# Attention scores in the array's row halves, grouped values in its column halves, steps by query tile

## The chip, the core and the metric

The kernel runs on one core of a Trainium2 chip. The metric is the time of one execution on the device in microseconds (us). The core's engines each run their own queue of instructions in order and wait for each other on semaphores: PE (TensorE, the matmul array), VectorE (DVE in the profile), ScalarE (ACT), GpSimd (POOL), and SyncE (SP), whose queue issues nearly all loads. Matmul results land in PSUM, eight banks of 128 partitions by 512 floats. An f32 matmul is two passes over the array and so two MATMUL records in the trace.

## The reference

A transformer block: modulation of the input by a condition vector, two attentions side by side, and a mixture of 32 experts, followed by a second block with a retention layer and a feed-forward net. The change touches the two attentions over 256 queries and 512 keys:

```python
def gqa_attention(q, k, v, q_block):          # 8 heads of 64, 2 key/value heads
    def block(qi):
        s = jnp.einsum('bhgqd,bkhd->bhgqk', qi, k) * scale
        p = jax.nn.softmax(s, axis=-1)
        return jnp.einsum('bhgqk,bkhd->bqhgd', p, v)
...
def diff_attention(q, k, v, lam, sub_g, lambda_init, q_block):   # 4 heads, two score maps of 64
    def block(qi):
        s = jnp.einsum('bhcqd,bkhcd->bhcqk', qi, k) * scale
        p = jax.nn.softmax(s, axis=-1)
        a = p[:, :, 0] - lam * p[:, :, 1]
        return jnp.einsum('bhqk,bkhe->bqhe', a, v)
    ...
    o = rms_norm(o, sub_g) * (1.0 - lambda_init)
```

The eight grouped heads are four pairs here: pair `c` holds head `c` of key/value head 0 and of key/value head 1 (`j`). Each head has 64 dimensions, so a score contracts over 64 only, half the array's 128 rows; a grouped value product has 64 output rows, half its columns.

## The kernel before

`attention_block` does everything from the first normalisation to the router. Weights come in 1 MB tiles; each is split by ScalarE (`hi`, line 141) and VectorE (`lo`, line 142), and a projection is three matmuls per tile (`hi,hh`, `hi,hl`, `lo,hh`, line 593). A scheduler orders each engine's instructions from their priorities and dependencies; the source gives the priorities. PE works through the projections of the difference attention (`kbT`, `vd`, `qd`) in the gaps of the grouped attention.

`attend` runs over `heads`, in the grouped attention eight (`c`, `j`), in the difference attention four. Step `i` issues the scores of head `i` (both query tiles `qt`), the transposes of head `i-1`, and the value product of head `i-2`, and calls `ada_step` (below). A grouped score uses rows `64*j` to `64*j+63` of `qT` and `kaT` and goes to bank `sc` (one bank). A difference score runs over 128 rows, with a `qd` in which the other half is zero (line 453, memset on GpSimd); two of them per query tile go to banks from the common pool `bank()`. `soft` takes the row maximum on VectorE (line 509), the exponential with sum on ScalarE (line 512), the reciprocal on VectorE (line 513). Grouped heads are scaled on ScalarE (line 530); difference heads are combined on VectorE (lines 536 to 538). The transposes go to bank `t`, and ScalarE copies them to `pTs` (line 520). The grouped value product writes `o[:64, :256]` (line 555), 256 columns over four key chunks, and ScalarE copies it into `mix` (line 557). The difference product (line 560) is followed by a sum of squares, an inverse root on VectorE (`rst`, `rsy`, lines 156 to 165), its spread over the columns (lines 289, 290), and `mix` on VectorE (line 568).

`Columns` is the modulation stream: it turns the condition vector into shifts and scales. A group is eight loads of 512 KB (two buffers); VectorE multiplies each by its column and adds it to `acc` (line 190 for the first, line 192 for the others), and after the eighth a `finish` sums over the partitions with eight one-column matmuls on PE (line 203) into bank `s`, from which VectorE adds the bias (line 205). There is one `acc` tile. `ada_step` hands out these steps over 30 places in the attention, at a low priority:

```python
for _ in range(min(len(todo) - slots[1] + slots[1] * slots[0] // ADA_PLACES, len(todo))):
    with tc.high_priority(offset=-LOW1):
        todo.pop(0).step((lambda: bank1("s")) if todo else None)
```

Behind the attention stand the output projection `w_o` (line 238), the router, and the experts (line 918), whose weights SyncE loads as soon as PE has freed their tiles.

Of the kernel before, what the change touches and what calls it, by code (L numbers as in the profile page):

```python
# [8 lines left out]
F32 = mybir.dt.float32  # L9
# [284 lines left out]
def attention_block(tc, g):  # L294
# [4 lines left out]
    with ExitStack() as es:  # L299
# [151 lines left out]

        qd = g.hp.tile([128, 4, 2, 256], F32, tag="h2", name="qd")
        nc.gpsimd.memset(qd, 0.0)
# [45 lines left out]
        pend = {}  # L499

        def scores(qa, ka, kind):
            b = bank1("sc") if kind == "g" else bank()
            pe.matmul(out=b, lhsT=qa, rhs=ka, start=True, stop=True)
            return b
# [11 lines left out]
        def transposed(p, pT, qt):  # L516
            b = bank1("t")
            for k in range(4):
                pe.transpose(out=b[:, k * 128:(k + 1) * 128], in_=p[:, k * 128:(k + 1) * 128], identity=g.ident)
            s.copy(out=pT[:, :, qt * 128:(qt + 1) * 128], in_=b.rearrange("p (k q) -> p k q", k=4))  # L520

        def stage_scores(heads, i):
            kind, c, j = heads[i]
            out = []
            for qt in range(2):
                qs = slice(qt * 128, (qt + 1) * 128)
                if kind == "g":
                    r = slice(64 * j, 64 * j + 64)
                    p, z = soft(scores(qT[r, c, qs], kaT[r, :], kind))
                    s.activation(out=p, in_=p, func=ACTF.Copy, scale=z)  # L530
                else:
                    pz = []
                    for m in range(2):
                        pz.append(soft(scores(qd[:, c, m, qs], kbT[:, c], kind)))
                    (p, z), (p1, z1) = pz
                    v.tensor_tensor(out=z1, in0=z1, in1=nlam, op=ALU.mult)
                    v.tensor_scalar(out=p, in0=p, scalar1=z, scalar2=None, op0=ALU.mult)
                    v.scalar_tensor_tensor(out=p, in0=p1, scalar=z1, in1=p, op0=ALU.mult, op1=ALU.add)
                out.append(p)
            pend[i] = out  # L540

        def stage_T(heads, i):
            pT = at.tile([128, 4, 256], F32, tag="pTs", name="pTs")
            for qt, p in enumerate(pend[i]):
                transposed(p, pT, qt)
            pend[i] = pT

        def stage_pv(heads, i):
            kind, c, j = heads[i]
            pT = pend.pop(i)  # L550
# [1561 lines left out]
```

## Time and profile before

| | us |
|---|---|
| median of 3 runs | 2090.07 |
| least and greatest | 2088.04, 2090.89 |
| the profiled execution | 2090.91 |
| its span in the trace | 2089.2 |
| first grouped score | 100.68 |
| first difference score | 192.30 |
| PE busy over the span | 1951.1 (93%) |

The trace is of one execution. Times of rows count from the start of its span, in us; a row of the timeline gives start, duration, engine, line, operation, output <- inputs, tile shape and count, and in brackets how long the engine had been idle before and what ended that. Durations of pipelined matmuls overlap: the step from one start to the next is what one costs. The chain of work that ended last lies in the second block, so the stretch of the change is read from the tables of stretches and the timelines.

### The profile page before, as it was taken

What the parts mean: (1) busy time and instruction counts of PE and PEld (TensorE: products, weight loads), DVE (VectorE), ACT (ScalarE), POOL (GpSimd) and SP (SyncE); (2) the same over time, 40 slices, a digit from 0 to 9 for tenths busy, and PEclk for the clock granted to TensorE, in tenths of its full rate; (3) what the DMA queues carried; (4) which work ended last, traced back from release to release, by engine and by line L of the source; (5) the groups of instructions that cost most, each with busy time, mean ns of one, the idle gap of its engine ahead of it and who ended that gap; (6) DMA issues with size and microseconds to landing.
All of it is one profiled execution on the core that took longest, in us unless ns stands there. A gap on an engine that the chain in (4) does not pass through costs nothing. (4 is left out here: it accounts for less than half of the span.)

```text
span 2089.2 us, 29010 instructions
## 1 busy us (share of the span) xinstructions
PE 1951.1 (93%) x11166; PEld 1246.5 (60%) x11166; DVE 1125.1 (54%) x2378; ACT 648.0 (31%) x1135; POOL 59.2 (3%) x92
## 2 busy tenths in 40 slices
PE   6999989999999989999998997999999999899998
PEld 3856844444333333332333326888999999599998
DVE  5865765132222212221222127999898978768863
ACT  3464311000000000000000004446677645256542
POOL 0000000000000000000000000000001002100000
PEclk9999989999999999999999998999999999799999
DMA  8656559999999999999999994667857778655651
GB/s 315 223 162 221 207 224 365 405 379 375 421 421 421 421 421 420 422 421 421 421 421 421 421 414 160 228 221 273 301 213 249 271 286 296 211 186 192 223 182 61
DMA packets 101757, 643.40 MB, mean 308 GB/s; under 512 B 11584, under 2 KB 12880, under 8 KB 34288
## 3 DMA queue, kind: packets, MB, share of 16 engines
q1 hardware_dynamic: 94176, 613.46, 75.1%
q0 software_dynamic: 6624, 26.76, 3.8%
q8 instruction: 89, 1.46, 0.3%
q10 hardware_dynamic: 816, 1.30, 0.2%
q14 instruction: 52, 0.43, 0.1%
HBM read 626.79 MB, written 14.68 MB: 307 GB/s over the span
## 5 line engine op out<-in xcount | busy, mean ns | idle before, releaser
L918 PE MATMUL hc<-w,xe 128*64 128x512 f32 (+1 forms) x2008 | 476.1, 598 | 54.1 <-DMA w<-in_w_in_dram 54.0
L918 PEld LDWEIGHTS hc<-w,xe 128*64 128x64 f32 (+1 forms) x2008 | 142.4, 138 | 375.3 <-issue 218.4
L142 DVE TENSOR_TENSOR lo<-w,hi 128x1024 fp32r<-128x1024 f32 x238 | 289.1, 1219 | 75.0 <-ACT hi L141 74.0
L141 ACT CAST hi<-w 128x1024 fp32r<-128x1024 f32 x238 | 249.0, 1049 | 253.0 <-PE b L241 156.7
L240 PE MATMUL b<-h2h,hi 128*128 128x256 f32 x896 | 254.6, 285 | 10.7 <-ACT h2h L1729 9.1
L938 DVE COPY hs<-hc 128x512 f32<-128x512 f32 x33 | 22.8, 691 | 448.8 <-PE hc L918 448.8
L241 PE MATMUL b<-h2l,hi 128*128 128x256 f32 x896 | 254.5, 285 | 0.2
L242 PE MATMUL b<-h2h,lo 128*128 128x256 f32 x896 | 253.9, 284 | 0.0
L918 PE MATMUL yb<-w,hb 128*64 128x512 f32 (+1 forms) x1024 | 252.6, 604 | 0.5 <-DMA w<-in_w_out_dram 0.5
L240 PEld LDWEIGHTS b<-h2h,hi 128*128 128x128 f32 x896 | 169.8, 190 | 13.3 <-ACT h2h L1729 9.3
L241 PEld LDWEIGHTS b<-h2l,hi 128*128 128x128 f32 x896 | 169.7, 190 | 4.0 <-issue 1.1
L242 PEld LDWEIGHTS b<-h2h,lo 128*128 128x128 f32 x896 | 169.7, 190 | 0.4 <-issue 0.4
L936 ACT COPY hs<-hc 128x512 f32<-128x512 f32 x33 | 19.3, 585 | 464.2 <-PE hc L918 464.2
L918 PEld LDWEIGHTS yb<-w,hb 128*64 128x64 f32 (+1 forms) x1024 | 66.8, 137 | 127.5 <-issue 119.5
L192 DVE SCALAR_TENSOR_TENSOR acc<-w,c,acc 128x1024 f32<-128x1024 f32 x77 | 98.4, 1278 | 12.0 <-DMA w<-in_ada_w_dram 11.4
L240 PE MATMUL b<-ah,hi 128*128 128x256 f32 x352 | 100.3, 286 | 0.0
L242 PE MATMUL b<-ah,lo 128*128 128x256 f32 x352 | 99.9, 284 | 0.2 <-DVE lo L142 0.2
L241 PE MATMUL b<-al,hi 128*128 128x256 f32 x352 | 99.4, 283 | 0.0
L981 ACT COPY ys<-yb 64x512 f32<-64x512 f32 (+1 forms) x32 | 18.5, 578 | 243.1 <-PE yb L918 243.1
L900 PEld LDWEIGHTS gb<-S,h 128*128 128x128 f32 x544 | 66.7, 197 | 37.2 <-issue 25.8
L1009 DVE TENSOR_TENSOR yacc<-sc,yacc 128x512 f32<-128x512 f32 x68 | 46.7, 688 | 66.5 <-PE sc L1007 66.5
L900 PE MATMUL gb<-S,h 128*128 128x128 f32 (+1 forms) x544 | 74.9, 289 | 1.2 <-DVE S L891 1.2
(523 smaller groups left out, 3061.1 us busy)
## 6 DMA issues: line engine op xcount, KB each, us to landing
w<-in_w_in_dram SPq DMA_DIRECT2D x252, 1024.0 KB, 13.1
w<-in_w_out_dram SPq DMA_DIRECT2D x128, 1024.0 KB, 14.5
w<-in_ffn_up_dram SPq DMA_DIRECT2D x44, 1024.0 KB, 5.0
w<-in_ada_w_dram SPq DMA_DIRECT2D x72, 512.0 KB, 5.0
w<-in_ret_w_in_dram SPq DMA_DIRECT2D x24, 1024.0 KB, 5.1
w<-in_ffn_down_dram SPq DMA_DIRECT2D x22, 1024.0 KB, 5.1
w<-in_w_ada_dram SPq DMA_DIRECT2D x32, 512.0 KB, 4.5
w<-in_ada_w_dram POOLq DMA_DIRECT2D x24, 512.0 KB, 4.8
```

Of the source, the lines that this page charges most:

```text
L141: self.nc.scalar.copy(out=hi, in_=w)
L142: self.nc.vector.tensor_tensor(out=lo, in0=w, in1=hi.bitcast(F32), op=ALU.subtract)
L192: v.scalar_tensor_tensor(out=self.acc, in0=w, scalar=cc, in1=self.acc, op0=ALU.mult, op1=ALU.add)
L240: pe.matmul(out=o, lhsT=w[0][:, sl], rhs=a[0][:, k], start=first, stop=False)
L241: pe.matmul(out=o, lhsT=w[0][:, sl], rhs=a[1][:, k], start=False, stop=False)
L242: pe.matmul(out=o, lhsT=w[1][:, sl], rhs=a[0][:, k], start=False, stop=last)
L900: g.got = pe.matmul(out=b[:, k * 128:k * 128 + n], lhsT=g.h2[:, t, d * 128:(d + 1) * 128], rhs=S[:, t, :n], start=(t == 0), stop=(t == 1))
L918: g.got = pe.matmul(out=on, lhsT=x, rhs=w[:, n * 512:n * 512 + 512], start=first, stop=last)
L936: s.copy(out=h, in_=hc[e][n])
L938: v.tensor_copy(out=h, in_=hc[e][n])
L981: s.copy(out=o, in_=i)
L1009: v.tensor_tensor(out=y, in0=b, in1=y, op=ALU.add)
```

## The change

The scores of both heads of a pair (grouped), or of both score maps of a head (difference), are issued one after the other on the array's upper and lower 64 rows and into different banks: grouped ones to `sc` and `s`, difference ones to two banks of the common pool. `qd` has no zero half any more, and one copy per query tile fills it. A step is now a query tile of a pair or head: `attend` runs eight steps per kind, with the transposes one step and the value product two steps behind. The grouped value product alternates between the column halves for `j` = 0 and 1, 128 query columns each; `mix` is copied once per pair. The difference product has 128 columns twice instead of 256 once. Each head's transposed weights have a tile of their own. `ada_step` is called with other numbers: 17 of 30 places in the grouped attention (15 before) and 10 in the difference attention (9 before). Lines from about 600 on are eight lower after the change.

```diff
--- before.py
+++ after.py
@@ -448,9 +448,7 @@
         qT, kbT, vd = (g.mw.tile([128, 2048], F32, tag="w", name=n) for n in ("qT", "kbT", "vd"))
         o24 = qT[:, 1024:].rearrange("p (i j t) -> p i j t", i=2, j=2)
         qT = qT[:, :1024].rearrange("p (c t) -> p c t", c=4)
-
-        qd = g.hp.tile([128, 4, 2, 256], F32, tag="h2", name="qd")
-        nc.gpsimd.memset(qd, 0.0)
+        qd = g.hp.tile([128, 4, 256], F32, tag="h2", name="qd")
         kbT, vd = (x.rearrange("p (c t) -> p c t", c=4) for x in (kbT, vd))
         va = pa.tile([128, 4, 128], F32, name="va")
         kaT = pa.tile([128, 512], F32, name="kaT")
@@ -496,12 +494,7 @@
         mix = g.sqp.tile([128, 8, 256], F32, tag="sq", name="mix")
         at = es_a.enter_context(tc.tile_pool(name="at", bufs=2))
 
-        pend = {}
-
-        def scores(qa, ka, kind):
-            b = bank1("sc") if kind == "g" else bank()
-            pe.matmul(out=b, lhsT=qa, rhs=ka, start=True, stop=True)
-            return b
+        bo = {}
 
         def soft(b):
 
@@ -513,51 +506,49 @@
             v.reciprocal(out=z, in_=z)
             return p, z
 
-        def transposed(p, pT, qt):
+        def transposed(p, j):
             b = bank1("t")
             for k in range(4):
                 pe.transpose(out=b[:, k * 128:(k + 1) * 128], in_=p[:, k * 128:(k + 1) * 128], identity=g.ident)
-            s.copy(out=pT[:, :, qt * 128:(qt + 1) * 128], in_=b.rearrange("p (k q) -> p k q", k=4))
-
-        def stage_scores(heads, i):
-            kind, c, j = heads[i]
-            out = []
-            for qt in range(2):
-                qs = slice(qt * 128, (qt + 1) * 128)
-                if kind == "g":
-                    r = slice(64 * j, 64 * j + 64)
-                    p, z = soft(scores(qT[r, c, qs], kaT[r, :], kind))
+            pT = at.tile([128, 4, 128], F32, tag=f"pT{j}", name="pTs")
+            s.copy(out=pT, in_=b.rearrange("p (k q) -> p k q", k=4))
+            return pT
+
+        def stage_scores(kind, c, qt):
+
+
+            q, ka = (qT, kaT) if kind == "g" else (qd, kbT[:, c])
+            bs = [bank1("sc"), bank1("s")] if kind == "g" else [bank() for _ in range(2)]
+            for j, b in enumerate(bs):
+                r = slice(64 * j, 64 * j + 64)
+                pe.matmul(out=b, lhsT=q[r, c, qt * 128:(qt + 1) * 128], rhs=ka[r], start=True, stop=True)
+            pz = [soft(b) for b in bs]
+            if kind == "g":
+                for p, z in pz:
                     s.activation(out=p, in_=p, func=ACTF.Copy, scale=z)
-                else:
-                    pz = []
-                    for m in range(2):
-                        pz.append(soft(scores(qd[:, c, m, qs], kbT[:, c], kind)))
-                    (p, z), (p1, z1) = pz
-                    v.tensor_tensor(out=z1, in0=z1, in1=nlam, op=ALU.mult)
-                    v.tensor_scalar(out=p, in0=p, scalar1=z, scalar2=None, op0=ALU.mult)
-                    v.scalar_tensor_tensor(out=p, in0=p1, scalar=z1, in1=p, op0=ALU.mult, op1=ALU.add)
-                out.append(p)
-            pend[i] = out
-
-        def stage_T(heads, i):
-            pT = at.tile([128, 4, 256], F32, tag="pTs", name="pTs")
-            for qt, p in enumerate(pend[i]):
-                transposed(p, pT, qt)
-            pend[i] = pT
-
-        def stage_pv(heads, i):
-            kind, c, j = heads[i]
-            pT = pend.pop(i)
-            o = bank1("o" if kind == "g" or c % 2 == 0 else "sc")
+                return [p for p, _ in pz]
+            (p, z), (p1, z1) = pz
+            v.tensor_tensor(out=z1, in0=z1, in1=nlam, op=ALU.mult)
+            v.tensor_scalar(out=p, in0=p, scalar1=z, scalar2=None, op0=ALU.mult)
+            v.scalar_tensor_tensor(out=p, in0=p1, scalar=z1, in1=p, op0=ALU.mult, op1=ALU.add)
+            return [p]
+
+        def stage_pv(kind, c, qt, pTs):
+            if qt == 0:
+                bo[c] = bank1("o" if kind == "g" or c % 2 == 0 else "sc")
+            o, qs = bo[c], slice(qt * 128, (qt + 1) * 128)
             if kind == "g":
-
                 for k in range(4):
-                    pe.matmul(out=o[:64, :256], lhsT=va[:, k, 64 * j:64 * j + 64], rhs=pT[:, k], start=(k == 0), stop=(k == 3))
-                r = slice(64 * j, 64 * j + 64)
-                s.copy(out=mix[r, c], in_=o[:64, :256])
+                    for j in range(2):
+                        r = slice(64 * j, 64 * j + 64)
+                        pe.matmul(out=o[r, qs], lhsT=va[:, k, r], rhs=pTs[j][:, k], start=(k == 0), stop=(k == 3))
+                if qt == 1:
+                    s.copy(out=mix[:, c], in_=o[:, :256])
             else:
                 for k in range(4):
-                    pe.matmul(out=o[:, :256], lhsT=vd[:, k, 128 * c:128 * c + 128], rhs=pT[:, k], start=(k == 0), stop=(k == 3))
+                    pe.matmul(out=o[:, qs], lhsT=vd[:, k, 128 * c:128 * c + 128], rhs=pTs[0][:, k], start=(k == 0), stop=(k == 3))
+                if qt == 0:
+                    return
                 o2, osb = (o24[:, c % 2, j] for j in range(2))
                 s.activation(out=o2, in_=o[:, :256], func=ACTF.Square)
                 s.activation(out=osb, in_=o[:, :256], func=ACTF.Copy, scale=g.subln)
@@ -567,16 +558,19 @@
                 spread(g, at, r, o[:, 256:])
                 v.tensor_tensor(out=mix[:, 4 + c], in0=osb, in1=o[:, 256:], op=ALU.mult)
 
-        def attend(heads):
-            n = len(heads)
-            for i in range(n + 2):
-                if i < n:
-                    stage_scores(heads, i)
-                if 0 <= i - 1 < n:
-                    stage_T(heads, i - 1)
-                if 0 <= i - 2 < n:
-                    stage_pv(heads, i - 2)
-                ada_step(2 if i % 2 else 1)
+        def attend(kind):
+
+
+            pend, pT = {}, {}
+            for i in range(10):
+                if i < 8:
+                    pend[i] = stage_scores(kind, *divmod(i, 2))
+                if 0 <= i - 1 < 8:
+                    pT[i - 1] = [transposed(p, j) for j, p in enumerate(pend.pop(i - 1))]
+                if i >= 2:
+                    stage_pv(kind, *divmod(i - 2, 2), pT.pop(i - 2))
+                if kind == "g" or i % 2:
+                    ada_step(2 if i % 4 else 1)
 
         def project(n, toks):
 
@@ -632,7 +626,7 @@
                             in0=qo[t].rearrange("p (j c d) -> p j c d", j=2, d=64),
                             in1=bc(r[:, 8 * t:8 * t + 8], 2, 64).rearrange("p (j c) d -> p j c d", j=2), op=ALU.mult)
             to_T(q2, qT[:, :, t * 128:(t + 1) * 128])
-        attend([("g", c, j) for c in range(4) for j in range(2)])
+        attend("g")
 
         bs = project(512, (0, 1, 2, 3))
         for t in range(4):
@@ -657,15 +651,13 @@
             for c in range(4):
                 pe.transpose(out=b[:, c * 128:(c + 1) * 128], in_=q2[:, c * 128:(c + 1) * 128], identity=g.ident)
             b = b.rearrange("p (c q) -> p c q", c=4)
-            for m in range(2):
-                r = slice(64 * m, 64 * m + 64)
-                s.copy(out=qd[r, :, m, t * 128:(t + 1) * 128], in_=b[r])
+            s.copy(out=qd[:, :, t * 128:(t + 1) * 128], in_=b)
 
         for i in range(20, 24, 2):
             t = g.hw.tile([128, 2, 2048], F32, tag="h", name="hw")
             for j in range(2):
                 ws.stream.load(i + j, t[:, j])
-        attend([("d", h, 0) for h in range(4)])
+        attend("d")
         for i in (17, 18, 24):
             ws.stream.ahead(i, g.mw)
         ws.stream.extend(g.mw, 3, 25, 13 + 32 * 12 - 1)
```

Three places in the order of the instructions. A row has its engine's line, operation, output <- input, shape, and a count where it repeats. First PE around the second finish of the modulation stream (`ones,acc`); before, bank `s` serves finishes alone:

```order
L593 MATMUL b<-lo,hh 128x512
L503 MATMUL sc<-kaT,qT 128x512
L519 MATMUL t<-ident,p 128x128 x4
L203 MATMUL s<-ones,acc_854 128x1 x8
L593 MATMUL b<-hi,hl 128x512
```

After, a score into `s` stands close behind the finish, without the score of its pair in front of it:

```order
L587 MATMUL b<-hi,hl 128x512
L203 MATMUL s<-ones,acc_858 128x1 x8
L587 MATMUL b<-hi,hh 128x512
L587 MATMUL b<-lo,hh 128x512
L524 MATMUL s<-kaT,qT 128x512
```

The score into `s` has moved behind the finish; its partner into `sc` is elsewhere in the queue.

Second, PE at the fourth finish and the first difference scores (`kbT,qd`), before:

```order
L203 MATMUL s<-ones,acc_1135 128x1 x8
L658 MATMUL t<-ident,qo 128x128 x4
L503 MATMUL b<-kbT,qd 128x512 x2
L658 MATMUL t<-ident,qo 128x128 x4
L503 MATMUL b<-kbT,qd 128x512 x6
L519 MATMUL t<-ident,p 128x128 x4
```

And after:

```order
L203 MATMUL s<-ones,acc_1134 128x1 x8
L652 MATMUL t<-ident,qo 128x128 x4
L524 MATMUL b<-kbT,qd 128x512 x2
L652 MATMUL t<-ident,qo 128x128 x4
L524 MATMUL b<-kbT,qd 128x512 x3
L512 MATMUL t<-ident,p 128x128 x4
L524 MATMUL b<-kbT,qd 128x512
L549 MATMUL o<-pTs,vd 128x128 x4
```

The first two scores stay together; later ones no longer come six in a row, but singly and in runs among transposes and value products.

Third, VectorE before the last `mix` of the difference attention (`rst`, `rsy`: the inverse root; `acc`: the modulation stream), before:

```order
L165 TENSOR_SCALAR rsy<-rst,rsy 128x1 x2
L289 TENSOR_SCALAR dgs<-ident,rsy 128x128 x2
L205 TENSOR_TENSOR mod_94<-s,pvt 128x8
L190 TENSOR_SCALAR acc_1684<-w,c_99 128x1024
L568 TENSOR_TENSOR mix<-qT,sc 128x256
L676 TENSOR_TENSOR rsc<-mod_93,pvt 128x8
```

And after:

```order
L289 TENSOR_SCALAR dgs<-ident,rsy 128x128 x2
L192 SCALAR_TENSOR_TENSOR acc_1669<-w,c_99,acc_1669 128x1024
L559 TENSOR_TENSOR mix<-qT,o 128x256
L192 SCALAR_TENSOR_TENSOR acc_1669<-w,c_99,acc_1669 128x1024
L156 TENSOR_SCALAR rsx<-sc 128x2
```

The modulation stream's accumulations have moved forward: the group that began just ahead of the last `mix` now has two of its line-192 rows ahead of it, around the `mix` before the last.

## Rows read from the trace of the kernel before

**Rows 1.** Stretches: length, busy of PE, PEld, DVE, ACT, POOL, granted clock, DMA share, GB/s.
```profile
100.50:167.00 66.50, 66.50 (x277) 36.71 (x276) 40.33 (x64) 39.13 (x80) 0.00 (x0) 1.00 0.46 144
...
192.00:232.50 40.50, 39.49 (x161) 26.20 (x162) 35.33 (x116) 21.30 (x52) 0.00 (x0) 0.94 0.48 175
...
360.00:400.00 40.00, 39.63 (x177) 16.05 (x178) 10.22 (x22) 3.92 (x7) 0.00 (x0) 1.00 1.01 420
```

**Rows 2.** Timeline of PE around the first finish and the first score.
```profile
90.25 2.75 PE L203 MATMUL s<-ones,acc 128*128 128x1 f32 x16 [1.44 <-DVE acc L192]
92.86 0.77 PE L593 MATMUL b<-hi,hl 128*128 128x512 f32 x1
93.44 0.63 PE L593 MATMUL b<-hi,hh 128*128 128x512 f32 x1
93.86 0.63 PE L593 MATMUL b<-lo,hh 128*128 128x512 f32 x1
...
100.68 1.12 PE L503 MATMUL sc<-kaT,qT 64*128 64x512 f32 x2
101.73 0.51 PE L593 MATMUL b<-hi,hh 128*128 128x512 f32 x1
102.08 0.40 PE L593 MATMUL b<-lo,hh 128*128 128x512 f32 x1
102.31 0.39 PE L593 MATMUL b<-hi,hl 128*128 128x512 f32 x1
```

**Rows 3.** Timeline of PE at a grouped value product.
```profile
113.17 1.51 PE L555 MATMUL o<-pTs,va 128*64 128x256 f32 x6
114.61 0.51 PE L593 MATMUL b<-hi,hh 128*128 128x512 f32 x1
```

**Rows 4.** Timeline of PE in the experts, column halves.
```profile
599.96 1.94 PE L918 MATMUL hc<-w,xe 128*64 128x512 f32 x8 [0.55 <-DMA w<-in_w_in_dram]
```

**Rows 5.** Timeline of VectorE: first and last accumulation of two groups.
```profile
93.20 0.75 DVE L190 TENSOR_SCALAR acc<-w,cs 128x1024 f32<-128x1024 f32 x1
...
121.30 1.28 DVE L192 SCALAR_TENSOR_TENSOR acc<-w,cs,acc 128x1024 f32<-128x1024 f32 x1
...
161.38 0.74 DVE L190 TENSOR_SCALAR acc<-w,cs 128x1024 f32<-128x1024 f32 x1
...
180.81 1.28 DVE L192 SCALAR_TENSOR_TENSOR acc<-w,cs,acc 128x1024 f32<-128x1024 f32 x1 [0.39 <-DMA w<-in_w_ada_dram]
```

**Rows 6.** Timeline of PE from the fourth finish into the difference attention.
```profile
187.71 1.84 PE L203 MATMUL s<-ones,acc 128*128 128x1 f32 x16
...
192.30 3.78 PE L503 MATMUL b<-kbT,qd 128*128 128x512 f32 x4 [0.72 <-ACT qd L662]
195.88 1.06 PE L658 MATMUL t<-ident,qo 128*128 128x128 f32 x4
...
202.86 0.60 PE L519 MATMUL t<-ident,p 128*128 128x128 f32 x4
203.29 2.16 PE L503 MATMUL b<-kbT,qd 128*128 128x512 f32 x4
...
205.72 1.02 PE L503 MATMUL b<-kbT,qd 128*128 128x512 f32 x2
206.59 0.68 PE L560 MATMUL o<-pTs,vd 128*128 128x256 f32 x2
```

**Rows 7.** Groups of VectorE's instructions from 192 to 240.2 us, the accumulations.
```profile
L192 DVE SCALAR_TENSOR_TENSOR acc<-w,c,acc 128x1024 f32<-128x1024 f32 x7 | 8.9, 1278 | 0.0
```

**Rows 8.** Timeline of VectorE, the last mix of the difference attention.
```profile
240.12 0.41 DVE L568 TENSOR_TENSOR mix<-qT,sc 128x256 f32<-128x256 f32 x1
```

**Rows 9.** Timeline of PE in the output projection; seven products are 14 passes.
```profile
245.11 3.27 PE L238 MATMUL b<-mix,w 128*128 128x256 f32 x14
```

**Rows 10.** Timeline of VectorE in the router, an accumulation in the inverse root.
```profile
268.59 1.28 DVE L192 SCALAR_TENSOR_TENSOR acc<-w,c,acc 128x1024 f32<-128x1024 f32 x1
```

**Rows 11.** Longest waits of SyncE's load queue: in total, times, longest.
```profile
SPq L109 <- PE hc L918: 401.1, 251, 17.5
```

## Prediction

> **What bounds the kernel now.** I read the table of stretches first, for who is busy where [rows 1]. In the grouped attention (100.5 to 167 us) PE is busy all of its 66.5 us; VectorE and ScalarE are busy for 40 and 39 us and DMA for 0.46. In the difference attention (192 to 232.5) PE stands at 39.5 of 40.5 and VectorE at 35.3. From 360 to 400, among the experts, the DMA share is 1.01 at 420 GB/s: they are a stream of weights, not of arithmetic. So time saved on PE in the first 190 us is worth something only if what follows starts earlier, and a shift there should pass through the experts one to one, since the bytes behind it stay the same; the order of the instructions behind the router is unchanged.
>
> Next I read PE's instructions at the place where attention begins [rows 2]. Two projection chains and one finish of the modulation stream stand around the first score. At 90.25 PE has idled 1.44 us for VectorE's last `acc`; then the finish takes 2.6 us and the projections go at half pace, 0.42 from 93.44 to 93.86. The first score starts at 100.68, the next instruction at 101.73: 1.05 us for a product of two passes. In the difference attention, where the neighbour has the full array, two such passes take 0.87 us (205.72 to 206.59) [rows 6]. The 0.2 us between them is what a change between a half and the full array costs.
>
> **PE's sum for the grouped part, first score to fourth finish.** Prices, as the step from one start to the next (the durations include the pipeline): a score 0.85, a projection 0.2275 (0.23 between the last two lines of [rows 2]), a transpose 0.107 (four from 202.86 to 203.29, [rows 6]), a 256-column value product 0.427 (six passes, three products, take 1.44 with a change at the end, [rows 3]), a column of a finish 0.23 (16 passes, eight columns, 1.84, [rows 6]), a change of array 0.2. Before: 16 scores 13.7, 56 changes 11.2, 32 value products 13.7, 80 transposes 8.6, 162 projections 36.9, 24 finish columns 5.6; together 89.5. The trace has 187.71 + 1.84 - 100.68 = 88.9 [rows 2, 6], so PE is filled and the prices hold.
>
> After: the scores come in row pairs and value products in column pairs, but the order on PE keeps only three of eight score pairs next to each other; the second score of the others stands behind a finish or projections. That leaves 13 score times (11.1 us), 64 half-length products that pair up (64 x 0.107 = 6.9), 51 changes (10.2), transposes 8.6, 165 projections 37.5, 32 finish columns 7.4: 81.7 us, 7.8 less. No row shows two row halves at once. The bounds are 0.85 (both at once) and 1.7 us (one after the other) a pair. Column halves are seen in the experts: eight passes of 128x64 take 1.94 us, 0.24 each [rows 4], against 0.43 for one alone; I take the pairing for both, because the nearest row shows it for columns. Without row pairing the sum is 84.2, without column pairing 88.5.
>
> The tiling rule speaks against splitting pairs. The 0.2 us of [rows 2, 6] is the price at each change here. The Trainium skill ("TensorEngine Tiling (Array Packing)", Key Properties) says that changing the tiling mode drains the engine, and this trace agrees, 1.05 against 0.87 us. By that the sum stands as written; if changes were free it would be 71.5.
>
> **The start.** The finish moves behind the first score pairs, with three projections. From 100.68 the 1.44 of idling and the 2.6 of finish leave, and three projections: 96.0. The operand that VectorE splits for the projections still stands behind the same `acc`, so some of that wait stays; I take 96, bounds 94 to 99. PE alone would reach the fourth finish at 96 + 81.7 - 1.8 = 176, 11.8 us before 187.71.
>
> **The modulation stream.** This is the term that decides. Each finish now needs its eight accumulations, and the second score of steps 2, 4 and 7 writes bank `s`, which the finish also uses, so PE's queue has the finish ahead of them. Behind the waiting finish everything on PE waits: projections, transposes, value products. A group's eight accumulations took 29.4 us when they lay among softmax steps (93.20 to 121.30 + 1.28) and 20.7 when only their loads paced them (161.38 to 180.81 + 1.28) [rows 5]. After: the first finish comes 6.1 us of PE behind the first score, 102.3 at full clock; with the half clock that [rows 2] shows behind such a wait, about 104, and VectorE starts the next group at 105. Groups two and three lie among softmax; I take the middle, 25, plus 2 us for finish and hand-over, twice: 159. The fourth stands behind the last softmax: 20.7 gives 180. Two more stalls of PE at the finishes with their slower passes are worth about 1 us each: 182. So the difference attention starts 5.7 us earlier, with bounds -11.8 (all groups at 20.7, PE decides) and +0.8 to +10 (29.4 for two or three groups).
>
> **The difference attention.** Its start: four projected-query copies become two (0.58 us saved where PE waited for both), and the first two scores, 3.58 us at half clock (192.30 to 195.88, [rows 6]), lie next to each other on their halves, 1.8 less: -2.4. Later PE saves scores (16 x 0.87 to about 11) and pays 18 changes x 0.2 = 3.6, a wash of 0.7; PE is not last there. VectorE is: between first reduce and last mix it holds the softmax, four rsqrt chains and accumulations. Seven of these stand in the window before [rows 7], one ahead of the first reduce; after, nine stand behind it: three more at 1.28, +3.8 (bounds 0, if they fall into VectorE's gaps, and 5). The last mix ended at 240.53 [rows 8].
>
> **Behind the last mix.** After it stand 40 products of w_o instead of 36: four at 3.27/7 = 0.45, +1.8 [rows 9]; eight mod transposes (8 x 0.107) move ahead of it: -0.9. In the router's rsqrt chain stood an `acc` of 1.28 [rows 10]; it has moved forward: -1.3. Copies on ScalarE fall from 8 to 4 and the memset on GpSimd goes; both engines have room [rows 1], nothing.
>
> **Sum.** -5.7 - 2.4 + 3.8 + 0.9 - 1.3 = -4.7 us at the experts' start. There SyncE's queue waits 401 us in all for tiles that PE frees [rows 11], so loads cannot run further ahead and the shift passes on. The profiled execution took 2090.91 us, 0.84 above the median of 2090.07; the same difference on the median gives 2085.4.
>
> **Rivals.**
> A. PE decides, the stream keeps up: every group needs 20.7 to 23 us. For it: PE wants 24.7, 25.4 and 23.5 us between the finishes, close to that. Against: 29.4 was seen. d starts 11.8 earlier: -10.8, 2079.3.
> B. The halves do not run together, rows or columns, since pairs share the queue with projections. PE needs about 91 us: 96 + 91 - 1.8 = 185, 2.5 earlier, and the 1.8 of the first d scores is lost: -2.5 - 0.6 + 3.8 - 0.4 = +0.3, 2090.4, no change. The column row speaks against it [rows 4]; nothing speaks for rows.
> C. Slower. The finish on bank `s` becomes the pace: groups take 29.4 us as in the first one, PE stands in front of each finish with everything behind it and runs at half clock afterwards. Two such groups: 105 + 2 x 31.4 + 20.7 = 188.5, with the clock 190.5, +2.8; three: 197, +9.5. With -2.4 + 3.8 - 0.4 this is +3.8 to +10.5; I take +6, 2096. It decides from a mean of about 27 us a group on. For it: the one tile for `acc` and two buffers for loads. Against: DMA is at half share in the stretch [rows 1].
> D. The pairs save time, but the experts' stream hides it, because its first loads wait for something else: 2090. [rows 11] speaks against it.
>
> **How the numbers follow.** Forecast 0.40, A 0.20, B 0.17, C 0.18, D 0.05. A measurement of this kernel can tell about 0.2%, 4.2 us, from no change: faster means under 2085.9, slower over 2094.3. The forecast itself spans 2082 to 2089, about 0.6 of it faster; with A and a little of the rest, faster is 0.45. B, D and what is left of the forecast and C give same 0.38, slower 0.17. The range goes from A's middle to C's: 2079 to 2095.5.
>
> **What would show it.** First score near 96; score pairs with starts a few ns apart where they are adjacent; value pairs 0.24 a pass; the fourth finish at 182 with PE idle for `acc` ahead of the second to fourth (A: 176, no idling; C: over 190); last mix at 236; the expert stream from 360 on unchanged, only earlier. The prediction is wrong if the three extra accumulations in the difference attention cost nothing, if row halves exclude one another, or if experts do not start earlier when attention ends earlier.

## The result: slower by half a per cent

The median went from 2090.09 us to 2099.51 us (six runs each), a ratio of 1.0053 with a 95% interval of 1.0027 to 1.0079. The forecast was 2085.4, faster; the time lies above the whole range. The profiled execution of the changed kernel took 2100.24 us, its span 2098.5.

The grouped part came out close to what was foretold. These rows of PE answer to [rows 2]: the first score pair, the second pair, a score alone, the first finish, and a value product.

```profile
94.20 0.69 PE L524 MATMUL sc<-kaT,qT 64*128 64x512 f32 x1
94.21 0.69 PE L524 MATMUL s<-kaT,qT 64*128 64x512 f32 x1
94.74 0.59 PE L524 MATMUL sc<-kaT,qT 64*128 64x512 f32 x1
94.75 0.59 PE L524 MATMUL s<-kaT,qT 64*128 64x512 f32 x1
95.26 0.50 PE L587 MATMUL b<-hi,hh 128*128 128x512 f32 x1
...
97.21 1.12 PE L524 MATMUL sc<-kaT,qT 64*128 64x512 f32 x2 [0.29 <-ACT p L505]
97.88 1.12 PE L524 MATMUL s<-kaT,qT 64*128 64x512 f32 x2
98.93 0.66 PE L512 MATMUL t<-ident,p 128*128 128x128 f32 x4
...
100.25 1.12 PE L524 MATMUL sc<-kaT,qT 64*128 64x512 f32 x2
101.31 1.95 PE L203 MATMUL s<-ones,acc 128*128 128x1 f32 x16
...
113.02 1.09 PE L544 MATMUL o<-pTs,va 128*64 128x128 f32 x14
114.04 0.50 PE L587 MATMUL b<-hi,hh 128*128 128x512 f32 x1
```

The two row halves of a pair start 0.01 us apart, and the pair takes 1.06 us (94.20 to 95.26), as much as one score did. The second pair came apart: its `s` half waited for its bank and began 0.67 later, and the pair took 1.72 (97.21 to 98.93). Value products in both column halves cost 1.02/14 = 0.073 a pass here, against 0.24 a pass of twice the columns before [rows 3].

The difference part did not. PE again, answering to [rows 6]:

```profile
180.92 1.95 PE L203 MATMUL s<-ones,acc 128*128 128x1 f32 x16 [1.55 <-DVE acc L192]
183.82 0.63 PE L652 MATMUL t<-ident,qo 128*128 128x128 f32 x4 [0.95 <-DVE qo L477]
185.12 2.08 PE L524 MATMUL b<-kbT,qd 64*128 64x512 f32 x4 [0.68 <-ACT qd L654]
187.13 1.11 PE L652 MATMUL t<-ident,qo 128*128 128x128 f32 x4
189.26 3.77 PE L524 MATMUL b<-kbT,qd 64*128 64x512 f32 x6 [1.02 <-ACT qd L654]
...
194.01 2.07 PE L524 MATMUL b<-kbT,qd 64*128 64x512 f32 x2
196.02 2.07 PE L549 MATMUL o<-pTs,vd 128*128 128x128 f32 x8
198.02 3.66 PE L524 MATMUL b<-kbT,qd 64*128 64x512 f32 x8
...
204.73 1.12 PE L524 MATMUL b<-kbT,qd 64*128 64x512 f32 x2
```

A single score (`x2`) takes 2.07 us at 194.01 and 1.12 at 204.73: PE is at half clock until about 201. Before, twelve passes of scores from 197.60 on took 0.44 each (5.26 us to the next row at 202.86 in [rows 6]), which is full clock:

```profile
197.60 5.42 PE L503 MATMUL b<-kbT,qd 128*128 128x512 f32 x12 [0.67 <-ACT qd L662]
```

The table of stretches says the same, to be read beside [rows 1] (the last three columns are the granted clock, the DMA share and GB/s): the clock went from 1.00 to 0.95 in the grouped part and from 0.94 to 0.80 in the difference part.

```profile
100.50:167.00 66.50, 66.50 (x376) 45.32 (x376) 40.46 (x60) 34.82 (x70) 0.00 (x0) 0.95 0.54 182
192.00:232.50 40.50, 36.52 (x161) 24.23 (x160) 32.54 (x102) 15.69 (x40) 0.00 (x0) 0.80 0.44 158
```

On VectorE the last mix, which answers to [rows 8], stands 2.9 us later than before:

```profile
243.00 0.42 DVE L559 TENSOR_TENSOR mix<-qT,sc 128x256 f32<-128x256 f32 x1 [1.56 <-PE sc L290]
```

The accumulations of line 192 between first difference score and last mix are nine instead of six; with one of line 190 in each, ten instead of seven. ([Rows 7] shows seven, because its window takes in one that begins at 192.20, just before the first difference score.)

```profile
L192 DVE SCALAR_TENSOR_TENSOR acc<-w,c,acc 128x1024 f32<-128x1024 f32 x9 | 11.5, 1278 | 0.0
```

In the same stretch VectorE (third busy time) works 44.6 us instead of 41.2 and idles 13.3 instead of 6.6, before and after:

```profile
192.30:240.11 47.81, 47.07 (x206) 32.93 (x206) 41.22 (x137) 21.03 (x51) 0.00 (x0) 0.95 0.53 193
...
185.12:243.00 57.88, 52.87 (x231) 35.74 (x232) 44.60 (x142) 19.55 (x49) 0.00 (x0) 0.80 0.52 188
```

| stage, profiled executions, us | before | after |
|---|---|---|
| first grouped score | 100.68 | 94.20 |
| fourth finish on PE | 187.71 | 180.92 |
| first difference score | 192.30 | 185.12 |
| first difference score to last mix | 47.8 | 57.9 |
| last mix | 240.12 | 243.00 |
| experts' start | 286.91 | 288.88 |
| end of the span | 2089.2 | 2098.5 |

So 7.2 us were won and 10.1 lost before the last mix. Pairing the same PE instruction in both traces gives the rest: +2.0 at the experts' start, +5.1 from 320 on, +5.9 through the experts, +8.0 from 1280, +9.3 at the end. In the first step, 3.1, the clock shows again. The stretch of 300 to 320 us has 0.91 before:

```profile
300.00:320.00 20.00, 19.99 (x88) 8.04 (x84) 6.14 (x17) 6.51 (x10) 0.55 (x1) 0.91 0.51 192
```

and 0.74 after:

```profile
300.00:320.00 20.00, 19.99 (x70) 7.60 (x68) 6.30 (x17) 5.00 (x8) 0.00 (x0) 0.74 0.53 223
```

### The profile page after: what moved, and what is told of

Read it like the earlier page. It is cut to its first block, busy times and chain, and to the rows that moved or that the text cites. A ratio compares the mean times of both kernels' runs of the same rounds, so it can differ in the third digit from the quotient of the medians.

```text
span 2098.5 us, 29178 instructions
## 1 busy us (share of the span) xinstructions
PE 1957.3 (93%) x11262; PEld 1255.5 (60%) x11262; DVE 1125.6 (54%) x2378; ACT 643.7 (31%) x1129; POOL 57.4 (3%) x91
## 5 line engine op out<-in xcount | busy, mean ns | idle before, releaser
L910 PE MATMUL hc<-w,xe 128*64 128x512 f32 (+1 forms) x2008 | 476.3, 598 | 54.8 <-DMA w<-in_w_in_dram 54.6
L1001 DVE TENSOR_TENSOR yacc<-sc,yacc 128x512 f32<-128x512 f32 x68 | 46.7, 689 | 66.4 <-PE sc L999 66.4
```

The source lines that it names most:

```text
L910: g.got = pe.matmul(out=on, lhsT=x, rhs=w[:, n * 512:n * 512 + 512], start=first, stop=last)
L1001: v.tensor_tensor(out=y, in0=b, in1=y, op=ALU.add)
```

## The experiments

The runs of one kernel spread by 6 to 26 us, and the trace is of one of them, so both are shown. The ratio is to the kernel before on the same chip; it is not the quotient of the medians (for e1 that would be 1.0020, for e4 1.0033), so differences of 0.001 between ratios mean little. "d" is from first difference score to last mix, in the profiled execution; "clock" is the mean granted clock over all runs.

| kernel | median us | ratio, 95% interval | d | experts' start | clock |
|---|---|---|---|---|---|
| before, again (b2_before) | 2088.66 | 1.0000, 0.9973 to 1.0028 | 46.7 | 283.3 | 0.979 |
| after, again (a2_after) | 2101.81 | 1.0061, 1.0031 to 1.0092 | 57.2 | 291.1 | 0.971 |
| e1_d_old | 2093.88 | 1.0036, 1.0012 to 1.0060 | 50.8 | 281.8 | 0.975 |
| e2_g_old | 2091.52 | 1.0009, 0.9991 to 1.0026 | 47.5 | 283.9 | 0.978 |
| e3_d_fullrows | 2093.95 | 1.0033, 1.0013 to 1.0053 | 50.5 | 282.3 | 0.974 |
| e4_d_heads | 2096.49 | 1.0017, 0.9993 to 1.0040 | 50.8 | 283.9 | 0.973 |
| e5_hold | 2102.80 | 1.0073, 1.0047 to 1.0099 | 56.0 | 292.1 | 0.969 |
| e7_filler | 2095.24 | 1.0027, 1.0001 to 1.0052 | 50.5 | 292.8 | 0.975 |
| e8_scores_full | 2088.13 | 1.0001, 0.9979 to 1.0023 | 54.6 | 279.4 | 0.977 |
| e9_values_full | 2102.03 | 1.0058, 1.0039 to 1.0077 | 49.5 | 292.6 | 0.974 |
| e10_all_full | 2094.04 | 1.0026, 1.0005 to 1.0047 | 48.6 | 284.7 | 0.977 |
| e12_g_scores_full | 2092.38 | 1.0024, 1.0004 to 1.0044 | 54.9 | 281.4 | 0.975 |
| e11_full_hold | 2089.60 | 1.0006, 0.9984 to 1.0027 | 52.6 | 283.2 | 0.977 |

The times go with the clock, except for e9, which has the clock of e3 and takes 8 us longer. Within one kernel too, a run with a mean clock lower by 0.001 takes about 1.4 to 2 us longer in most of them.

**Each part alone.** e1 puts the difference attention back (`attend_h` and its helpers are those of before; the transposed weights of both heads share a tile for space):

```diff
-        attend("d")
+        attend_h([("d", h, 0) for h in range(4)])
```

> The grouped attention as changed, the difference attention as before (steps by head, scores over 128 rows with a zero half, value products of 256 columns). The traces of before and after show that the grouped part gains 7.2 us (first difference score 185.1 against 192.3) and the difference part loses 10 (first score to last mix 57.9 against 47.8 us). Theory S (the difference part's own change loses it): first score to last mix goes back to about 48 + 4 (three more accumulations stand there, since the order still has ten behind the first reduce), last mix near 237, the kernel 2087 to 2090. Rival G (the new grouped part pushes the accumulations and the loads into the difference part, whatever its form): first score to last mix stays at 55 to 58, the kernel stays at 2096 to 2100.

e2 puts the grouped attention back:

```diff
-        attend("g")
+        attend_h([("g", c, j) for c in range(4) for j in range(2)])
```

> The grouped attention as before, the difference attention as changed. Theory S: first difference score at about 192, first score to last mix about 54 (58 less the three accumulations that are not there), last mix near 246, the kernel 2098 to 2102. Rival G: the difference part needs 48 or less as before, the kernel 2086 to 2090.

Neither theory held as put. The new difference part alone needs 47.5 us, as before: by itself it loses nothing. The old one behind the new grouped part needs 50.8, with ten accumulations instead of seven. 57 us needs both parts new. What e2 has and the changed kernel has not is the clock: no wait stands ahead of its fourth finish, and its first pair runs at full clock.

```profile
189.01 1.13 PE L523 MATMUL b<-kbT,qd 64*128 64x512 f32 x4 [0.68 <-ACT qd L726]
```

The profiled execution of e1 was its quickest of ten runs, 2085.86, so its early experts' start stands for its best case.

**Row halves or steps.** e3 keeps the steps and takes the difference scores over 128 rows, with the zero half in `qd` again:

```diff
-                pe.matmul(out=b, lhsT=q[r, c, qt * 128:(qt + 1) * 128], rhs=ka[r], start=True, stop=True)
...
+                    pe.matmul(out=b, lhsT=qd[:, c, j, qs], rhs=ka, start=True, stop=True)
```

> As changed, but the difference scores run over 128 rows with the zero half again; steps by query tile stay. Rival R (the row halves cause the loss in the difference part, by changes of the array and by keeping PE at half clock from 187 to 201 us): first score to last mix falls from 58 to about 52, the kernel 2091 to 2094. Theory S with the steps as the cause: it stays within 2 us of 58 and the kernel within 2096 to 2101.

e4 keeps the row halves and goes by heads:

```diff
-        attend("d")
+        attend_h([("d", h, 0) for h in range(4)])
...
-                        pz.append(soft(scores_h(qd[:, c, m, qs], kbT[:, c], kind)))
+                        r = slice(64 * m, 64 * m + 64)
+                        pz.append(scores_h(qd[r, c, qs], kbT[r, c], kind))
+                    pz = [soft(b) for b in pz]
```

> As changed, but the difference attention goes by heads again (both query tiles in a step, so scores run four ahead), with row halves and 128-column value products kept. Theory S with the steps as the cause: first score to last mix falls to about 52, the kernel 2089 to 2093. Rival R: it stays at 56 to 58, the kernel 2096 to 2100.

Undoing either brings the length down by 6 to 7 us, and the clock is where both differ from the changed kernel. PE in e3 at the same place:

```profile
186.54 3.78 PE L529 MATMUL b<-kbT,qd 128*128 128x512 f32 x4 [0.72 <-ACT qd L661]
190.11 1.06 PE L657 MATMUL t<-ident,qo 128*128 128x128 f32 x4
191.84 4.56 PE L529 MATMUL b<-kbT,qd 128*128 128x512 f32 x10 [0.67 <-ACT qd L661]
```

It enters at half clock like the changed kernel, and ten passes over the whole array at 191.84 take 0.46 each: the clock is up 10 us sooner. In the stretch of 182 to 202 us the granted clock is 0.57 in the second profile of the changed kernel (a2, below):

```profile
182.00:202.00 20.00, 17.36 (x54) 9.11 (x56) 13.41 (x30) 6.01 (x15) 0.00 (x0) 0.57 0.80 309
```

and 0.83 in e3, at equal DMA:

```profile
182.00:202.00 20.00, 17.57 (x64) 9.66 (x65) 15.72 (x37) 9.47 (x23) 0.00 (x0) 0.83 0.79 308
```

PE is as busy in one as in the other, and both waited 1.54 us for the fourth finish; the edit between them is the row halves of the difference scores. e4, row halves by heads, lies between with 0.74 in the same stretch.

**Chance or kernel.** Both kernels once more:

> The changed kernel once more, unaltered, on the chip of the next three. The experiments so far, all with part of the difference attention as before, needed 47.5 to 50.8 us from first difference score to last mix, the changed kernel 57.9 with PE at half clock for most of 187 to 201 us. If the half clock belongs to the kernel (theory C), this profile shows 56 to 59 again and about 14 us of half clock between 180 and 205; if it was chance (rival Z), 50 to 52 and the kernel's median falls to that of the others.

> The kernel before once more, for the spread of one profile. First difference score to last mix 47 to 49; if the half clock at 300 to 320 us and behind 1240 us is a matter of phase, these places differ from the first profile by 2 to 4 us although nothing was changed.

The length of 57 us and the half clock belong to the changed kernel. The two profiles of before differ by 3.6 us at the experts' start with nothing changed, though, so single shifts of that size behind the attention prove little. Around 300 to 320 the second profile of before has the same 0.74 as the changed kernel, so the 3.1 us lost there in the first comparison need not be the change's. Paired like the first two, the second profiles give +7.8 at the experts' start, +6.2 at 350, +5.9 at the experts' end and +11.5 at the end of the span. Both pairs share 5 to 6 us from 350 to the experts' end. Behind that the unchanged kernel moves as much: its two profiles are 0.4 us apart at 350, 1.9 at the experts' end and 6.5 at the end.

**The accumulations.** e5 lets the sixth group wait for the last mix:

```diff
-                if kind == "g" or i % 2:
-                    ada_step(2 if i % 4 else 1)
+                if kind == "g":
+                    ada_step(2 if i % 4 else 1)
+                elif i == 9:
+                    with tc.issue_after(bo["last"].ins):
+                        ada_step(10)
```

> As changed, but the modulation stream's accumulations of the sixth group wait for the last mix: seven instead of ten stand between the first difference reduce and the last mix. Theory S2 (three accumulations of 1.28 us lengthen the difference part): its length falls by 3.5 to 4.5 us against the changed kernel on the same chip. Rival (they fall into gaps of VectorE): it falls by under 1.5. The kernel gains at most what the router does not lose again: an accumulation is back in its inverse root, 1.3 us.

Seven accumulations stood there instead of ten, VectorE was busy for 41.2 us instead of 44.1 between first difference score and last mix, and idle for 14.8 instead of 13.2 (a2): of 3.8 us only 1.2 came off the length. (The profiled execution of e5 was its quickest, 2086.29.) The rival holds. VectorE waits for PE instead. In the changed kernel its waits for scores are in this row, before (in [rows 7]'s view) they were 1.4; its waits for PE at the four mixes grew from 1.5 to 6.4, though those at 212 and 236 us stand at full clock:

```profile
L502 DVE TENSOR_REDUCE nm<-b 128x1 f32<-128x512 f32 x16 | 10.7, 682 | 3.8 <-PE b L524 3.8
```

**The waits of PE filled.** e7 puts products that are overwritten in front of the first four difference scores:

```diff
             for j, b in enumerate(bs):
+                if kind == "d" and c == 0:
+                    for _ in range(2):
+                        pe.matmul(out=b, lhsT=g.ident, rhs=kaT, start=True, stop=True)
```

> As changed, with eight extra products over the full array (two passes each, 0.87 us at full and 1.7 at half clock) in front of the first four difference scores, overwritten by these; they stand where PE waits for the last accumulation and for the projected queries. Theory C (PE's waits and the half-used array bring the clock down and the half clock lengthens the difference part): the clock is up before 190, first score to last mix falls from 58 to 51 to 54 in spite of up to 3 us more work. Rival: the length stays or grows, 58 to 62.

The difference part came out at 50.5 us with no half clock in it at all, in spite of the added work, as theory C has it. But in this profile PE did not wait for the fourth finish either (192.20, no idle time ahead of it), as in e2, so that the filler did it is not shown. In the median e7 is 6.6 us faster than a2; its profiled execution, one of its slower ones (2100.46), gained less, since its grouped part ran into half clock. PE in e7 after the first finish, no row with idle ahead of it:

```profile
107.97 0.78 PE L590 MATMUL b<-hi,hh 128*128 128x512 f32 x1
...
112.38 1.11 PE L512 MATMUL t<-ident,p 128*128 128x128 f32 x4
113.43 0.69 PE L547 MATMUL o<-pTs,va 128*64 128x128 f32 x2
114.05 2.07 PE L527 MATMUL sc<-kaT,qT 64*128 64x512 f32 x2
...
126.24 1.87 PE L547 MATMUL o<-pTs,va 128*64 128x128 f32 x14
128.04 0.51 PE L590 MATMUL b<-hi,hh 128*128 128x512 f32 x1
```

From the finish to the value product's end these rows take 20.1 us; the same rows of the changed kernel take 10.9 (103.11 to 114.04). The stretch of 103 to 128 us in e7:

```profile
103.00:128.00 25.00, 25.00 (x89) 13.65 (x87) 14.44 (x27) 12.82 (x28) 0.00 (x0) 0.59 0.25 85
```

PE is busy for all 25 us and gets 0.59 of the clock. The waits before it, 0.93 us at 96 and 0.26 at 101, are no longer than the 0.97 us that PE idled between 90 and 100 in a2, where the clock stays at 1.00 to 130. What the stretch has is scores in one row half at a time, short column-half products and transposes, with few whole-array projections between; but the changed kernel has the same rows there at full clock, so what brought it down in e7 is open.

**Which halves.** e8 takes all scores over 128 rows, the grouped ones with a zero half in the keys, and leaves the values in column halves:

```diff
-        kaT = pa.tile([128, 512], F32, name="kaT")
+        kaT = pa.tile([128, 2, 512], F32, name="kaT")
+        nc.gpsimd.memset(kaT, 0.0)
...
+                if kind == "g":
+                    pe.matmul(out=b, lhsT=q[:, c, qs], rhs=kaT[:, j], start=True, stop=True)
+                else:
+                    pe.matmul(out=b, lhsT=qd[:, c, j, qs], rhs=ka, start=True, stop=True)
```

In e8, and in e10, e11 and e12 below, the row maxima also have four buffers instead of two. In the changed kernel's traces, with two, no reduction waits for ScalarE to free one, so this is not what these kernels gain by.

> As changed, but all scores, grouped and difference, run over the array's 128 rows, with a zero half in the keys (grouped) or the queries (difference); the value products stay in the column halves. In the grouped part PE spends 16 x 0.87 on scores instead of 11 to 12 and saves the changes around them (about 5 us). Theory C2 (work in halves lets the clock fall and keeps it there: in the run with the filler PE was busy without a gap from 107 to 128 us and yet at half clock, over the same order of work that took half as long in the changed kernel): hardly any half clock between 100 and 240, difference part 50 to 51, experts' start at 278 to 282, mean clock 0.976 or more, kernel 2086 to 2092. Rival W (it is only the waits of PE for the modulation stream): half clock at 130, 150 and 180 as in the changed kernel.

e9 has grouped scores in row halves, difference scores over 128 rows, and the values over the whole array:

```diff
-                        pe.matmul(out=o[r, qs], lhsT=va[:, k, r], rhs=pTs[j][:, k], start=(k == 0), stop=(k == 3))
...
+                        pe.matmul(out=o[:, j * 256 + qt * 128:j * 256 + qt * 128 + 128], lhsT=va[:, k], rhs=pTs[j][:, k], start=(k == 0), stop=(k == 3))
```

> As changed, but the grouped value products use the whole array (128 columns of the values, half of the result unused, one after the other) and the difference scores 128 rows; grouped scores stay in row halves. PE's time for the grouped values goes from 64 x 0.107 plus changes to 64 x 0.214 and no change. If the column halves bring the clock down, the half clock at 130 and 150 goes; if the row halves do, it stays. Kernel 2088 to 2096.

e10 has both:

> Steps by query tile as changed, but nothing in halves: scores over 128 rows with zero halves, values over 128 columns. By PE's prices the grouped part needs 13.9 for scores, 13.7 for values and no changes, together 27.6, against 28.2 in the changed kernel (11.1, 6.9 and 10.2) and 38.6 before: the gain of the halves without them. Theory C2: no half clock between 100 and 240 but at the start of the difference part, experts' start at 277 to 281, mean clock 0.977 to 0.980, kernel 2080 to 2088. Rival: the kernel stays at 2092 or above, as the two with the new grouped part and the old difference part did.

e8 went back to the time of before, and its interval (0.9979 to 1.0023) lies below both of the changed kernel's (from 1.0027 and 1.0031 on). The clock is 1.00 at 130 and 150 us, where both profiles of the changed kernel have 0.83 to 0.87. First e8, then the changed kernel:

```profile
130.00:140.00 10.00, 10.00 (x53) 6.17 (x51) 8.51 (x15) 9.37 (x21) 0.00 (x0) 1.00 0.45 145
...
130.00:140.00 10.00, 10.00 (x44) 5.80 (x45) 6.96 (x13) 8.06 (x17) 0.00 (x0) 0.84 0.34 109
```

The column halves of the values are not the cause, and they are worth their place: against e3, e9 has the values over the whole array, and its projected queries are ready (their first transpose) 9.0 us later, 193.79 against 184.81; e10 against e8, 8.0 us later, 188.56 against 180.55. My sum for e10 was wrong in that, and its rival, 2092 or above, came true. In e9 the half clock at 130 us went, but 0.54 stood at 150 to 160, so neither place alone decides; its time, 2102.0, was above what I had expected. e9 and e10 ran on one chip and differ in the grouped scores (and the row maxima's buffers): every run of e9 (2098.5 to 2104.6) took longer than every run of e10 (2088.2 to 2097.6), by 8.0 us in the medians. So the row halves of the grouped scores cost time by themselves.

e12 is the fourth corner, e8 with the difference scores in row halves:

```diff
-                    pe.matmul(out=b, lhsT=qd[:, c, j, qs], rhs=ka, start=True, stop=True)
+                    pe.matmul(out=b, lhsT=qd[r, c, qs], rhs=ka[r], start=True, stop=True)
```

> As changed, but the grouped scores run over 128 rows with a zero half in the keys; the difference scores stay in row halves, the values in column halves. With the changed kernel (both in halves, mean 2101 to 2102 us), the one with full difference scores (2094 to 2096) and the one with both full (2088 to 2089) this is the fourth corner. If each half costs by itself, 2094 to 2097: the grouped halves cost 5 to 7 us by the clock in the grouped part (half clock at 130 and 150), the difference halves 5 to 7 by the clock in theirs (half clock from 182 to 200). If the difference halves alone hold the clock down, half clock from 180 to 200 and a length of 55 to 58 as in the changed kernel; if they need the grouped halves for that, 50 to 54.

With steps and column halves alike in all four, the ratios are 1.0001 (all scores full), 1.0024 (difference scores in halves, e12), 1.0033 (grouped scores in halves, e3) and 1.0053 to 1.0061 (both). Both together are clear of none. The two in the middle lie between, about 5 and 7 us above none, as if each cost something and the two added up; but their intervals overlap with each other and with both ends, so for the difference halves alone that is not shown, nor which is the dearer. The lengths of e12 and e8 do not tell them apart: 54.9 and 54.6, with eleven accumulations in each, although the clock in the stretch of 182 to 202 us is 0.70 in e12 and 0.92 in e8. VectorE idles 9.7 us in one and 9.4 in the other; why that is so long in e8, no run settles.

**A version that beats both** was not found. e11 is e8 with the accumulations held as in e5:

> All scores over 128 rows, values in column halves, and the modulation stream's sixth group held until the last mix, for a kernel that may beat both. With full scores the difference part had ten accumulations and took 54.7 us at full clock on VectorE; with three or four fewer its length should be 50 to 51, the last mix near 233, the experts' start at 276 to 280 and the kernel 2083 to 2088. Rival: the accumulations come back in the router and the experts' start stays at 279 to 281, the kernel 2087 to 2091.

Its last mix came 1.3 us sooner than e8's, but the accumulations came back in the router, and its time is that of before: the rival, with the experts' start at 283.2 even later than that had it.

## Why the prediction was wrong

- **Grouped part: right in its size, half right in its reason.** First score 94.2 (forecast 96), fourth finish 180.9 (forecast 182), first difference score 7.2 us earlier (the sum had 6.3; the other 1.8 of its 8.1 lies behind that score). PE idled 1.55 us for `acc` ahead of the fourth finish, but not ahead of the second and third. PE came there 6.8 us later than its sum at full clock (94.2 + 79.9 = 174.1). Of these 1.8 are idle time and at most 3.4 half clock (0.84 from 130 to 140, 0.85 from 150 to 160). The rest is work priced too low: the first finish, for one, came 7.1 us behind the first score, not 6.1.
- **Row halves together: right where the pair stands together,** 1.06 us. Single scores of a split pair cost 1.05, as priced.
- **Three more accumulations: right as work, wrong as length.** VectorE's busy time grew by 3.4 us between first difference score and last mix (41.2 to 44.6). But its idle time grew from 6.6 to 13.3 as well, and that the sum did not have; and held back in e5, the accumulations gave 1.2 us, not 3.8.
- **The step that failed is "PE is not last there", the wash of 0.7 in the difference attention.** The sum had this part 2.0 us longer (3.8 less 1.8); it was 10.1 longer. Behind the first two scores it was priced at full clock: the sum knew a half clock behind the waits for the finishes and gave two of these about 1 us each. In place of that stood 14 us of half clock from 187 to 201 and 7 more between 218 and 232, worth up to 7 and 3.4 us, as an estimate at half the pace. e3, which enters with the same wait and differs in the difference scores' row halves, is 6.7 to 7.4 us shorter than the two profiles of the changed kernel; 3.4 to 3.8 of that are there by the first mix. a2 and e5 show that the half clock belongs to the kernel, e2 that without the wait the new difference part loses nothing. How much of the 7 us at the later mixes is the clock and how much the order of work is not separated.
- **No term had the clock fall on a busy PE.** e7's grouped part shows 0.59 over 25 busy us, the changed kernel 0.84 from 130 to 140 after 30 us without idle time. Over all runs the mean clock is 0.971 against 0.979, 17 us of full clock in the span. The stretch of 183 to 250 us, 0.82 in both profiles of the changed kernel and 0.95 and 0.97 before, makes 9 to 10 of them. From 340 us on all four profiles have 0.98 or 0.99, so where the rest lies, in runs without a profile, no run settles.
- **One to one through the experts: not exact.** The profile was 6.7 us behind the sum at the experts' start (+2.0 against -4.7) and another 7.3 by the end, for which the sum had nothing. The two profiles of before start the experts 3.6 us apart and are 0.4 apart at 350. e8 starts the experts 3.9 us before the second profile of before, and is 1.8 ahead at 350 us and 0.6 at their end. Rival D had 0.05 for what turned out, in e8, to be more than half the gain.
- **Rival C,** slower because the modulation stream paces the finishes, gave a time of nearly the right size for the wrong reason. The finishes came 25.0, 27.3 and 27.2 us apart, near the point from which it was to decide, but the difference attention still began earlier, and the loss came after that.
- The drain that the Trainium skill names ("TensorEngine Tiling (Array Packing)", Key Properties) has its 0.2 us here too (1.06 us from 100.25 to 101.31 for a lone score, against 0.87 in [rows 6]). That all 51 changes of the sum cost as much is not shown: e10, without any in its scores and values, was not quicker than e8 with its column halves.

## What to carry to other kernels

Two products in the array's row halves do run in the time of one, but price the clock with it. Here, after the same wait of 1.54 us, the granted clock over the next 20 us was 0.57 with row halves and 0.83 with the same scores over the whole array. Compare the granted clock of each stretch before and after, and cost a stretch at both levels before calling PE "not last". When one part moves forward, list what slides into the gap on the next engine, here three accumulations.

## What had not been expected

PE fully busy for 25 us at 0.59 of its clock (e7, 103 to 128 us), over a mixture of half-array and short products; the changed kernel ran the same rows at 1.00 in its profile. The time of one kernel follows its mean clock closely from run to run, some 1.7 us for 0.001, so that six runs of the kernel before already lie within 2086.8 and 2091.8 us, and 31 in the series of a2, e5 and e7 within 2082.3 and 2102.6.
